# Attention scores of the first block: plain float32 products of 64 rows, or two float32r passes over 128 rows

## The chip, the cores and the metric

One core of a Trainium2 chip runs the whole program. The metric is device microseconds of one execution; the time of the kernel before is the median of three runs. TensorE multiplies, VectorE (DVE), ScalarE (ACT) and GpSimd (POOL) work on tiles of 128 partitions, and SyncE issues the loads of the weights.

## What is computed

Two stacks of layers over 256 rows of 1024 columns in float32. The first block has four layers: sliding-window attention (A), a mixture of three dilated attentions (B), an attention over the own block (C), and A again, each followed by a gated feed-forward net. The second block has two layers of another kind; its difference attention is computed as before. What the change touches is the score product of the first block, for one head:

```python
s = jnp.einsum('bnqhgd,bnkhd->bnhgqk', qb, kb) * (dh ** -0.5)   # dh = 64
s = jnp.where(ok[None, :, None, None], s, NEG)
m = s.max(-1)
p = jnp.exp(s - m[..., None])
o = jnp.einsum('bnhgqk,bnkhd->bnqhgd', p, vb) / ...
```

Layer A has 16 query heads on 4 key heads, layers B (three times, once for each dilation) and C have 16 query heads on 16 key heads.

## The kernel before

The 256 rows are two row tiles, t=0 and t=1, and each is a stream of work of its own: a Python generator that runs through all layers. The two take turns, the second four turns behind the first (LAG, line 54). A turn of a stream is half a unit of weights, which is six large products of 128x128 weights with 512 columns (mm3, line 399): inputs and weights are each split into a high and a low float32r part, and high-high, high-low and low-high are summed. ScalarE makes the high part of a weight and VectorE the low one (load, line 373), into eight buffers that both streams read. Beside a stream run small tasks, up to three a turn (spawn and turn, lines 430 and 438), among them the attention of four heads at a time. A scheduler of the framework then fixes the order of the instructions on each engine, and TensorE and the others follow that order.

A projection of 512 columns gives two blocks of 256, which are keys, values or queries of four heads (after, line 751). Keys and queries get the rotary step on VectorE (rope_apply, line 568), and then heads_t (line 580): two transposes of 128x128 into one PSUM bank and one eviction by ScalarE into a tile of 128 partitions by 2 x 128, two heads in the two halves of the partitions. In layer A each key head is first copied twice side by side (line 705), so that it lies in both halves, which makes four transposes and two evictions. In layer B the blocks come in the order v, k, q for each quarter and dilation, two to a chunk, so in every second group keys and queries come from one chunk.

scores (line 598) takes two PSUM banks, one for each parity of the four heads, and makes one plain float32 product with 64 rows for every head and 128 keys: four for t=0, which sees 128 keys, eight for t=1, which sees 256. The parities alternate. VectorE then adds the mask in PSUM and finds the maximum, ScalarE takes the exponential (attend, line 618), the probabilities are transposed (p_t, line 650) and multiplied with v. PSUM banks are named by tags: pj (3) for projections, ch (3) for scores and outputs, tp (2) for transposes. The tile v of a group is filled by ScalarE after a POOL memset of its column of ones (line 590); there are 7 buffers for v, 5 for keys (kt) and 3 for queries (qt).

Of the kernel before, what the change touches and what calls it, by code (L numbers as in the profile page):

```python
# [9 lines left out]
F32 = mybir.dt.float32  # L10
# [33 lines left out]
            bc=3, bcs=1, v=7, kt=5, qt=3, stg1=2, og=7, ob=3, ffg=4,  # L44
# [40 lines left out]
class Net:  # L85
# [45 lines left out]
    def own(self, name, shape, tag, dt=F32):  # L131
# [3 lines left out]
        pp = self.pl if tag in ("ho", "wx", "yt") else self.pp  # L135
# [462 lines left out]
    def scores(self, t, q, k, mask):  # L598

        nc = self.nc
        nk = (t + 1) * P
        svs = [self.bank().rearrange("p (h k) -> p h k", k=256)[:, :, :nk] for _ in range(2)]
        for a in range(2):
            for j in range(t + 1):
                for par in range(2):
                    nc.tensor.matmul(svs[par][:, a, j * P:(j + 1) * P], q(par, a), k(par, a, j), start=True, stop=True)  # L608
        for sv in svs:
# [3 lines left out]
            else:  # L613
                m = mask[:, None, (1 - t) * P:].to_broadcast([P, 2, nk])
                nc.vector.tensor_add(sv, sv, m)
        return svs

    def attend(self, t, qt, kt, mask, v, sink=None):
# [7 lines left out]
        svs = self.scores(t, lambda par, a: qt[par * 64:par * 64 + 64, a, :],  # L626
                          lambda par, a, j: kt(j, par + 2 * a), mask)
# [51 lines left out]
    def mixer_a(self, t, i, xt, st):  # L679
# [13 lines left out]
        def keys(ps):  # L693
# [7 lines left out]

            k2 = []
            for a in range(2):
                k = self.own("k2", [2, 2, 64], "stg1")
                nc.vector.tensor_copy(k, z[:, 128 * a:128 * a + 128].rearrange("p (h d) -> p h d", d=64)[:, :, None, :]
                                      .to_broadcast([P, 2, 2, 64]))
                k2.append(k.rearrange("p h a d -> p (h a d)"))
            yield from self.idle(W_QK_A)
            st["k", t] = [self.heads_t(k, "kt", 1.0) for k in k2]

        def queries(c, ps):
# [8 lines left out]
            qts = [self.heads_t(z, "qt", 0.125) for z in zs]  # L720
            yield
            def head(a):
                kvh = 2 * c + a
                h0 = 4 * kvh
                while ("k", 0) not in st:
                    yield
                o, nm = yield from self.attend(
                    t, qts[a], lambda jj, h: st["k", jj][kvh // 2][(h % 2) * 64:(h % 2) * 64 + 64, kvh % 2, :],
# [14 lines left out]
    def mixer_bc(self, t, i, xt, st, blocks, masks):  # L743
# [7 lines left out]
        def after(bl, ps):  # L751
# [20 lines left out]
            for zt, qq, g in qs:  # L772
                while any((a, qq, g, j) not in st for a in "kv" for j in range(t + 1)):
                    yield
# [741 lines left out]
```

## Time and profile before

| | |
|---|---|
| median of three runs | 2399.34 us (2399.07 to 2400.11) |
| the profiled execution | 2399.64 us |
| its span, first to last instruction | 2397.9 us |
| TensorE busy | 2357.5 us, 98% |
| VectorE, ScalarE, POOL busy | 1740.0, 1316.7, 150.3 us |

The span is read by stages. Attention of the four layers of the first block lies at about 35 to 110, 310 to 610, 820 to 925 and 1135 to 1215 us; the second block begins at about 1405 us.

### The profile page before, as it was taken

What the parts mean: (1) busy time and instruction counts of PE and PEld (TensorE: products, weight loads), DVE (VectorE), ACT (ScalarE), POOL (GpSimd) and SP (SyncE); (2) the same over time, 40 slices, a digit from 0 to 9 for tenths busy, and PEclk for the clock granted to TensorE, in tenths of its full rate; (3) what the DMA queues carried; (4) which work ended last, traced back from release to release, by engine and by line L of the source; (5) the groups of instructions that cost most, each with busy time, mean ns of one, the idle gap of its engine ahead of it and who ended that gap; (6) DMA issues with size and microseconds to landing.
All of it is one profiled execution on the core that took longest, in us unless ns stands there. A gap on an engine that the chain in (4) does not pass through costs nothing.

```text
span 2397.9 us, 34993 instructions
## 1 busy us (share of the span) xinstructions
PE 2357.5 (98%) x11664; PEld 1920.7 (80%) x11664; DVE 1740.0 (73%) x4260; ACT 1316.7 (55%) x2182; POOL 150.3 (6%) x433
## 2 busy tenths in 40 slices
PE   8999999999999999999999999999999999999999
PEld 6788878888788788887778877877888778788887
DVE  7755676666755767557775588987877889887876
ACT  5544456655444555444544445744677656545775
POOL 1100000000100001000010000100011201000111
PEclk9999999999999999999999999999999999999999
DMA  6366554444566645665366667567566686575663
GB/s 233 114 186 187 182 167 132 139 126 132 172 188 185 187 130 169 187 186 183 124 186 186 186 140 168 136 146 200 164 194 185 167 186 130 123 214 172 187 183 115
DMA packets 280117, 400.16 MB, mean 167 GB/s; under 512 B 20588, under 2 KB 205098, under 8 KB 279936
## 3 DMA queue, kind: packets, MB, share of 16 engines
q1 hardware_dynamic: 274784, 381.88, 55.2%
q0 software_dynamic: 5152, 16.05, 2.2%
q8 instruction: 92, 1.51, 0.3%
q14 instruction: 89, 0.73, 0.1%
HBM read 396.81 MB, written 1.05 MB: 166 GB/s over the span
## 4 chain that ended last, share of the span: by engine, by line
PE 86%; DVE 8%; DMA 3%; ACT 2%; issue 1%; ACTq 0%; DVEq 0%; SPq 0%
PE pj L404 21%; PE pj L406 21%; PE pj L405 21%; PE tp L451 4%; PE ch L404 4%; PE ch L406 4%; PE ch L405 4%; PE ch L608 3%; PE ch L646 2%; DVE w L395 2%; DMA raw<-in_w_in_dram 2%; PE tp L658 1%; ACT w L392 1%; DVE convy L997 1%; DVE x L545 0%
## 5 line engine op out<-in xcount | busy, mean ns | idle before, releaser
L395 DVE TENSOR_TENSOR w<-raw,w 128x512 fp32r<-128x512 f32 x1434 | 941.9, 683 | 467.2 <-ACT w L392 464.1
L392 ACT CAST w<-raw 128x1024 fp32r<-128x1024 f32 x728 | 758.9, 1043 | 659.8 <-PE pj L406 375.2
L404 PE MATMUL pj<-w,xth 128*128 128x512 f32 x2048 | 821.3, 402 | 4.9 <-DVE stg L716 1.9
L405 PE MATMUL pj<-w,xth 128*128 128x512 f32 x2048 | 804.0, 393 | 1.6 <-DVE w L395 1.5
L406 PE MATMUL pj<-w,xtl 128*128 128x512 f32 x2048 | 803.3, 393 | 1.6 <-DVE xtl L443 1.6
L404 PEld LDWEIGHTS pj<-w,xth 128*128 128x128 f32 x2048 | 385.7, 188 | 89.6 <-ACT xth L442 6.1
L406 PEld LDWEIGHTS pj<-w,xtl 128*128 128x128 f32 x2048 | 385.2, 188 | 86.3 <-DVE xtl L443 4.2
L405 PEld LDWEIGHTS pj<-w,xth 128*128 128x128 f32 x2048 | 386.1, 189 | 78.3 <-DVE w L395 4.1
L404 PE MATMUL ch<-w,fht 128*128 128x512 f32 x412 | 171.9, 417 | 1.8 <-ACT fht L442 1.8
L406 PE MATMUL ch<-w,fht 128*128 128x512 f32 x412 | 161.9, 393 | 0.0
L405 PE MATMUL ch<-w,fht 128*128 128x512 f32 x412 | 161.2, 391 | 0.0
L997 DVE SCALAR_TENSOR_TENSOR convy<-xc,ffn_cw,convy 128x128 f32<-128x128 f32 x352 | 100.7, 346 | 7.2 <-POOL ffn_hist L988 2.1
L406 PEld LDWEIGHTS ch<-w,fht 128*128 128x128 f32 x412 | 77.3, 188 | 18.4 <-DVE fht L443 0.8
L404 PEld LDWEIGHTS ch<-w,fht 128*128 128x128 f32 x412 | 77.4, 188 | 15.5 <-ACT fht L442 3.9
L405 PEld LDWEIGHTS ch<-w,fht 128*128 128x128 f32 x412 | 77.9, 189 | 12.2
L635 ACT ACTIVATE pexp<-ch,nm 128x128 f32<-128x128 f32 (+1 forms) x192 | 65.8, 421 | 38.2 <-DVE nm L630 23.9
L839 ACT ACTIVATE ffg<-pj 128x256 f32<-128x256 f32 x88 | 33.8, 384 | 86.0 <-PE pj L406 86.0
L994 ACT ACTIVATE convy<-xc,ffn_cw 128x128 f32<-128x128 f32 x176 | 72.8, 484 | 1.4
L646 PEld LDWEIGHTS ch<-v,pt 128*128 128x128 f32 x576 | 70.5, 191 | 2.9
L404 PE MATMUL pj<-w,fht 128*128 128x512 f32 x180 | 71.3, 396 | 0.0
L406 PE MATMUL pj<-w,fht 128*128 128x512 f32 x180 | 70.7, 393 | 0.0
L405 PE MATMUL pj<-w,fht 128*128 128x512 f32 x180 | 70.1, 389 | 0.0
(339 smaller groups left out, 2745.9 us busy)
## 6 DMA issues: line engine op xcount, KB each, us to landing
raw<-in_w_gate_up_dram SPq DMA_DIRECT2D x352, 256.0 KB, 3.3
raw<-in_w_in_dram SPq DMA_DIRECT2D x128, 512.0 KB, 5.0
raw<-in_w_down_dram SPq DMA_DIRECT2D x88, 512.0 KB, 3.6
raw<-in_ffn_w_up_dram SPq DMA_DIRECT2D x176, 256.0 KB, 3.3
raw<-in_b_w_qkv_dram SPq DMA_DIRECT2D x144, 256.0 KB, 3.1
raw<-in_ffn_w_down_dram SPq DMA_DIRECT2D x44, 512.0 KB, 4.5
raw<-in_a_w_qkv_dram SPq DMA_DIRECT2D x24, 512.0 KB, 4.5
raw<-in_c_w_qkv_dram SPq DMA_DIRECT2D x48, 256.0 KB, 3.3
```

The lines of the kernel that those rows point to most:

```text
L392: nc.scalar.copy(w[:, 0, :m], raw)
L395: self.last_low = e.tensor_sub(w[:, 1, s], raw[:, s], w[:, 0, s].bitcast(F32)).ins
L404: mm(ps, xh[:, k, :], wh[:, kk, cols], start=start, stop=False)
L405: mm(ps, xh[:, k, :], wl[:, kk, cols], start=False, stop=False)
L406: self.last_mm = mm(ps, xl[:, k, :], wh[:, kk, cols], start=False, stop=stop).ins
L451: self.nc.tensor.transpose(tp[:, b * P:(b + 1) * P], src[:, b * P:(b + 1) * P], self.ident)
L608: nc.tensor.matmul(svs[par][:, a, j * P:(j + 1) * P], q(par, a), k(par, a, j), start=True, stop=True)
L635: nc.scalar.activation(p[:, a, :(t + 1) * P], sv[:, a, :], AF.Exp, bias=n2[:, a:a + 1])
L646: nc.tensor.matmul(o[:, par + 2 * a, :], pts[par][:, a * (t + 1) + j, :], v(j, par + 2 * a), start=j == 0, stop=j == t)
L839: nc.scalar.activation(g, ps[:, :FFC], AF.Silu)
L994: nc.scalar.activation(y[:, a, :], xc[:, a, 4:], AF.Identity, bias=b[:, 0, c:c + 1], scale=w[:, h, c:c + 1])
L997: nc.vector.scalar_tensor_tensor(y[:, a, :], xc[:, a, o:o + P], w[:, j, c:c + 1], y[:, a, :], op0=OP.mult, op1=OP.add)
```

## The change

Queries and keys of the first block are now split into a high and a low float32r part too. For a head, the query tile holds its high part in the 64 partitions where the head's keys lie and its low part in the other 64, already scaled by 0.125 (queries_t). A key tile holds, for 256 keys of four heads, the high parts and the low parts, each in both halves of the partitions (keys_t): ScalarE writes the high part, VectorE the low one, and POOL copies both to the other half. A score is then the sum of two float32r products over all 128 rows, query tile with the high keys and query tile with the low keys, with 128 columns for t=0 and 256 for t=1. The parities come one after the other. One key tile holds both row tiles of a group, in two buffers; v gets 6 buffers for 7, and the doubled keys of layer A go. The second block's scores keep the old form under the name scores_64.

```diff
-            bc=3, bcs=1, v=7, kt=5, qt=3, stg1=2, og=7, ob=3, ffg=4,
+            bc=3, bcs=1, v=6, ks=2, qs=3, stg1=2, og=7, ob=3, ffg=4,
...
-    def heads_t(self, z, tag, scale):
-
+    def queries_t(self, z, scale):
+        nc = self.nc
         tp = self.blocks_t(z, 2)
-        zt = self.own("zt", [2, P], tag)
-        self.nc.scalar.activation(zt, tp, AF.Copy, scale=scale)
+        zt = self.own("zt", [2, 2, P], "qs", F32R)
+        for par in range(2):
+            here, there = self.half(par), self.half(1 - par)
+            nc.scalar.activation(zt[here, par], tp[here], AF.Copy, scale=scale)
+            nc.vector.scalar_tensor_tensor(zt[there, par], tp[here], scale, zt[here, par].bitcast(F32),
+                                           op0=OP.mult, op1=OP.subtract)
         return zt
+
+    def keys_t(self, z, ks, j):
+        nc = self.nc
+        tp = self.blocks_t(z, 2)
+        s = slice(j * P, (j + 1) * P)
+        for par in range(2):
+            here, there = self.half(par), self.half(1 - par)
+            nc.scalar.copy(ks[here, 0, par, :, s], tp[here])
+            nc.vector.tensor_sub(ks[here, 1, par, :, s], tp[here], ks[here, 0, par, :, s].bitcast(F32))
+            nc.gpsimd.tensor_copy(ks[there, :, par, :, s], ks[here, :, par, :, s])
+
+    def key_pair(self):
+        return self.own("ks", [2, 2, 2, 2 * P], "ks", F32R)
...
+    def scores(self, t, q, k, mask):
+        svs = self.score_banks(t)
+        for par, sv in enumerate(svs):
+            for a in range(2):
+                for part in range(2):
+                    self.nc.tensor.matmul(sv[:, a, :], q(par, a), k(par, a)[:, part, :(t + 1) * P],
+                                          start=part == 0, stop=part == 1)
+        return self.masked(t, svs, mask)
...
-            k2 = []
-            for a in range(2):
-                k = self.own("k2", [2, 2, 64], "stg1")
-                nc.vector.tensor_copy(k, z[:, 128 * a:128 * a + 128].rearrange("p (h d) -> p h d", d=64)[:, :, None, :]
-                                      .to_broadcast([P, 2, 2, 64]))
-                k2.append(k.rearrange("p h a d -> p (h a d)"))
             yield from self.idle(W_QK_A)
-            st["k", t] = [self.heads_t(k, "kt", 1.0) for k in k2]
+            self.keys_t(z, self.shared((i, "ks"), self.key_pair), t)
+            st["k", t] = True
...
-                    st["k", qq, g, t] = self.heads_t(z, "kt", 1.0)
+                    self.keys_t(z, self.shared((i, "ks", qq, g), self.key_pair), t)
+                    st["k", qq, g, t] = True
                 else:
-                    qs.append((self.heads_t(z, "qt", 0.125), qq, g))
+                    qs.append((self.queries_t(z, 0.125), qq, g))
```

## Rows read from the trace of the kernel before

**Rows 1.** The page's head: engine busy, share of the span, instructions.
```profile
span 2397.9 us, 34993 instructions
PE 2357.5 (98%) x11664; PEld 1920.7 (80%) x11664; DVE 1740.0 (73%) x4260; ACT 1316.7 (55%) x2182; POOL 150.3 (6%) x433
```

**Rows 2.** The page's chain that ended last, shares by engine.
```profile
PE 86%; DVE 8%; DMA 3%; ACT 2%; issue 1%; ACTq 0%; DVEq 0%; SPq 0%
```

**Rows 3.** Waits of TensorE: who waited <- releaser: us in total, times, longest.
```profile
PE pj L405 <- DVE w L395: 1.5, 2, 1.1
...
PE ch L608 <- ACT pexp L635: 0.2, 1, 0.2
```

**Rows 4.** Table by stage (layers B, C): stretch, busy us, granted clock, DMA.
```profile
310.00:600.00 290.00, 289.79 (x1690) 238.52 (x1689) 191.71 (x530) 171.60 (x369) 2.84 (x23) 1.00 0.45 138
820.00:920.00 100.00, 99.81 (x572) 82.34 (x573) 62.77 (x169) 59.10 (x119) 0.32 (x3) 1.00 0.47 145
```

**Rows 5.** Timeline, TensorE then VectorE, after a shared chunk: start, us, instruction [idle before].
```profile
353.99 0.61 PE L451 MATMUL tp<-ident,stg 128*128 128x128 f32 x4
...
354.67 0.39 PE L405 MATMUL pj<-w,xth 128*128 128x512 f32 x1
...
357.11 0.69 DVE L395 TENSOR_TENSOR w<-raw,w 128x512 fp32r<-128x512 f32 x1 [3.72 <-ACT w L392]
```

**Rows 6.** Timeline of TensorE around two score calls of t=1.
```profile
339.71 0.40 PE L406 MATMUL pj<-w,xtl 128*128 128x512 f32 x1
340.04 1.53 PE L608 MATMUL ch<-zt 64*128 64x128 f32 x16
...
341.83 0.39 PE L405 MATMUL pj<-w,xth 128*128 128x512 f32 x1
...
356.96 0.39 PE L406 MATMUL pj<-w,xtl 128*128 128x512 f32 x1
357.28 1.16 PE L608 MATMUL ch<-zt 64*128 64x128 f32 x16
...
358.71 0.39 PE L405 MATMUL pj<-w,xth 128*128 128x512 f32 x1
```

**Rows 7.** Lines and groups: counts, durations ns (min/median/max or mean), a wait.
```profile
L608 PE MATMUL ch<-zt x576: 272/272/373, 39.1 to 1196.8; 64*128 64x128 f32 x192
...
  ACT pexp L635: 3.7, 10
...
L451 PE MATMUL tp<-ident,k x16: 270/272/330, 25.0 to 1149.1; 128*128 128x128 f32 x16
...
L584 ACT ACTIVATE zt<-tp 128x256 f32<-128x256 f32 x88 | 32.1, 386 | 35.2 <-PE tp L451 33.5 <-PE ch L608 1.5 <-ACT zt L584 0.2
...
L443 DVE TENSOR_TENSOR fht<-tp,fht 128x256 fp32r<-128x256 f32 x104 | 43.4, 417 | 1.0 <-ACT fht L442 1.0
...
L442 ACT CAST fht<-tp 128x256 fp32r<-128x256 f32 x104 | 38.3, 368 | 10.0 <-PE tp L451 6.6 <-PE ch L406 1.9 <-PE pj L406 1.6
```

**Rows 8.** Timeline of TensorE around a score call of t=0.
```profile
323.59 0.40 PE L406 MATMUL pj<-w,xtl 128*128 128x512 f32 x1
323.92 0.71 PE L608 MATMUL ch<-zt 64*128 64x128 f32 x8
...
324.90 0.39 PE L405 MATMUL pj<-w,xth 128*128 128x512 f32 x1
```

**Rows 9.** Timeline of TensorE around four float32r products of 128 columns.
```profile
1576.13 0.40 PE L406 MATMUL pj<-w,xtl 128*128 128x512 f32 x1
1576.37 0.56 PE L1102 MATMUL ch<-ssact,pick 128*128 128x128 f32 x4
...
1577.04 0.40 PE L404 MATMUL pj<-w,xth 128*128 128x512 f32 x1
```

**Rows 10.** POOL's groups (busy, mean ns), and its waits from 310 to 600 us.
```profile
L395 POOL TENSOR_TENSOR w<-raw,w 128x512 fp32r<-128x512 f32 x22 | 28.6, 1319 | 553.0 <-ACT w L392 543.2 <-DVE eg L801 9.8
...
L166 POOL COPY maskt<-same 128x128 f32<-128x128 f32 x2 | 0.6, 289 | 50.7 <-DVE same L217 50.7
...
L278 POOL COPY r2cc<-r2cc 128x8 f32<-128x8 f32 x2 | 0.4, 184 | 0.4 <-ACT r2cc L277 0.4
...
POOL v L590 <- PE ch L646: 278.7, 16, 40.7
```

More of the change, by code (lines that the diff above doesn't have):

```diff
@@ L134, in own @@
             self.second_pool()
-        pp = self.pl if tag in ("ho", "wx", "yt") else self.pp
+        pp = self.pl if tag in ("ho", "wx", "ks", "yt") else self.pp
         return pp.tile([P] + shape, dt, name=name, tag=tag, bufs=BUFS[tag])
@@ L596, in v_tile, with masked @@
         return v
-    def scores(self, t, q, k, mask):
+    def masked(self, t, svs, mask):
         nc = self.nc
-        nk = (t + 1) * P
-        svs = [self.bank().rearrange("p (h k) -> p h k", k=256)[:, :, :nk] for _ in range(2)]
-        for a in range(2):
-            for j in range(t + 1):
-                for par in range(2):
-                    nc.tensor.matmul(svs[par][:, a, j * P:(j + 1) * P], q(par, a), k(par, a, j), start=True, stop=True)
         for sv in svs:
@@ L613, in scores, with score_banks, scores_64 @@
             else:
-                m = mask[:, None, (1 - t) * P:].to_broadcast([P, 2, nk])
+                m = mask[:, None, (1 - t) * P:].to_broadcast([P, 2, (t + 1) * P])
                 nc.vector.tensor_add(sv, sv, m)
         return svs
+    def score_banks(self, t):
+        return [self.bank().rearrange("p (h k) -> p h k", k=256)[:, :, :(t + 1) * P] for _ in range(2)]
+    def scores(self, t, q, k, mask):
[6 more added lines that the diff above has]
+        return self.masked(t, svs, mask)
+    def scores_64(self, t, q, k):
+        svs = self.score_banks(t)
+        for a in range(2):
+            for j in range(t + 1):
+                for par in range(2):
+                    self.nc.tensor.matmul(svs[par][:, a, j * P:(j + 1) * P], q(par, a), k(par, a, j),
+                                          start=True, stop=True)
+        return self.masked(t, svs, None)
     def attend(self, t, qt, kt, mask, v, sink=None):
@@ L624, in attend @@
         ps = []
-        svs = self.scores(t, lambda par, a: qt[par * 64:par * 64 + 64, a, :],
-                          lambda par, a, j: kt(j, par + 2 * a), mask)
+        svs = self.scores(t, lambda par, a: qt[:, par, a, :], lambda par, a: kt(par + 2 * a), mask)
         for par, sv in enumerate(svs):
@@ L719, in queries @@
             yield from self.idle(W_QK_A)
-            qts = [self.heads_t(z, "qt", 0.125) for z in zs]
+            qts = [self.queries_t(z, 0.125) for z in zs]
             yield
@@ L1138, in diff_attn @@
             ps, ls = [], []
-            svs = self.scores(t, lambda m, a: qt[64 * m:64 * m + 64, 2 * hp + a, :],
-                              lambda m, a, j: st["dk", j][64 * m:64 * m + 64, 2 * hp + a, :], None)
+            svs = self.scores_64(t, lambda m, a: qt[64 * m:64 * m + 64, 2 * hp + a, :],
+                                 lambda m, a, j: st["dk", j][64 * m:64 * m + 64, 2 * hp + a, :])
             for sv in svs:
```

10 lines of the change are left out of this document (7 added, 3 removed).

## The prediction

> **What bounds the kernel now.** I read the page's busy line and its chain first. TensorE is busy for 98% of a span of 2397.9 us [rows 1], and 86% of the chain that ended last is TensorE's own work [rows 2]. What TensorE waits for is small: of the waits that bear on this change the longest sum is 1.5 us, on the weights' low parts, and the scores wait 0.2 us in all [rows 3]. In the largest attention stage TensorE is busy 289.79 of 290 us, VectorE 191.71 and ScalarE 171.60, at a granted clock of 1.00 [rows 4]. So a saving counts here if it shortens what TensorE issues, and an addition on the other engines costs only where TensorE, which works in a fixed order, comes to wait for it.
>
> A busy TensorE overstates one instruction: records overlap. The unit is therefore what a burst inserts between the large products: from the start of the last 512-column product before it to the start of the second one after it, less two of their steps. Their step is 2.29 us for ten, from 354.67 to 356.96, so 0.229 us [rows 5, 6].
>
> **The price of the scores before.** The trace holds 576 records of score products in the first block [rows 7]; a plain float32 product leaves two, so these are 288 products: 24 calls for rows t=0 with 4 and 24 for t=1 with 8. A t=0 call inserts 324.90 - 323.59 - 0.458 = 0.85 us [rows 8]. A t=1 call inserts 358.71 - 356.96 - 0.458 = 1.29 us where nothing is late, and 341.83 - 339.71 - 0.458 = 1.66 us where it is [rows 6]. Eight more records thus cost 0.44 us, 0.055 us each, while eight alone cost 0.85: some 0.41 us of every call is entering and leaving. I read this as pairs that run beside each other in the two halves of the rows, with a toll at either edge. Both kinds of t=1 call are frequent, so I take the middle, 1.47 us, and keep both ends.
>
> **The price after.** Each call becomes 8 products over all 128 rows, t=0 with 128 columns and t=1 with 256. The nearest row is the second block's line 1102: four float32r products, 128 rows by 128 columns, insert 1577.04 - 1576.13 - 0.458 = 0.45 us, 0.113 each, with no toll [rows 9]. That also speaks against a penalty for a narrow float32r product: it costs half of a 512-column one. A t=0 call is then 8 x 0.113 = 0.90 us, 0.05 more than before: 24 x 0.05 = 1.2 us lost. For 256 columns there is no row. From below it is 0.113 (nothing cheaper than the narrow product), from above the straight line from 0.113 at 128 columns to 0.229 at 512, which is 0.152. Half of a 512-column step is 0.115; I take 0.12, near the low end, since 128 columns already cost more than a quarter of 512. A t=1 call is 8 x 0.12 = 0.96 us (0.90 to 1.22), and 24 x (1.47 - 0.96) = 12.2 us are won. With both sets of ends this term runs from 24 x (1.29 - 1.22) = 1.7 us to 24 x (1.66 - 0.90) = 18.2 us.
>
> The Trainium skill ("TensorE: Matmul & The Clock Gate", Back-to-back issue gap) gives about 81 ns for a sustained pair of weight load and 128-column product. By it a t=0 call would be an estimated 0.65 us and the sum 6 us better; the row of line 1102 shows 113 ns for this kernel's float32r form, and I go by the row.
>
> **Transposes.** The sliding-window layers no longer double their keys: 16 transposes of k [rows 7] become 8. At 0.113 us, the price of the narrow product (nearest row), this is 0.9 us won on TensorE, and eight copies go from VectorE.
>
> **What is added beside TensorE.** Key tiles: 2 x (1+12+4+1) = 36. Query tiles: 2 x (4+12+4+4) = 48. Before, 88 evictions of 386 ns served both [rows 7]. Now a key tile takes two ScalarE copies, two VectorE subtractions and two POOL copies, a query tile two ScalarE and two VectorE passes; every one has 64 partitions by 256 elements, POOL's 64 by 512. I price them by the 128-partition rows of the same length: 368 ns on ScalarE, 386 with a scale, 417 ns on VectorE [rows 7]. ScalarE: 72 x 0.368 + 96 x 0.386 - 88 x 0.386 = +29.6 us. VectorE: 168 x 0.417 = +70 us, less the eight copies. POOL: a copy of 128 elements takes 289 ns and one of 8 takes 184, so 512 elements are 184 + 504 x 0.875 = 625 ns; the far row is the two-operand 512-element subtraction at 1319 ns [rows 10]. 72 x 0.625 = 45 us.
>
> In the dilated stage 24 key tiles and 24 query tiles add 96 x 0.417 = 40 us to VectorE's 191.7 (80% of the stage) and some 18 us to ScalarE's 171.6 (65%) [rows 4]. Neither becomes the bound of the stage. As a load these are covered by TensorE; what matters is latency.
>
> **Latency, and who waits.** From a tile's transposes to its scores the way was one eviction. For keys it is now ScalarE, VectorE and POOL, and POOL serially for the two halves: 0.37 + 0.42 + 2 x 0.625 = 2.04 us, with handoffs some 2.2 us. The shortest cover is where keys and queries come from one chunk: transposes start at 353.99, the scores at 357.28 [rows 5, 6], 2.9 us after the last of four transposes. The second parity's scores come half a call later, 0.45 us more cover. VectorE is idle for 3.72 us there [rows 5], but it also has two query passes behind the key's two: 0.37 + 4 x 0.42 + handoffs = 2.3 us. So nothing is late where VectorE is free, and up to 0.7 us is late where a pair of weight subtractions (2 x 0.69 us) stands in front. On POOL the keys' copies stand behind the v tile's memsets, which wait for the attention product of an older group, 278.7 us in sum and up to 40.7 us at a time [rows 10]. With six v buffers for seven that wait ends one tile earlier in the ring; it harms only if the fixed order puts a key copy behind a memset whose release TensorE reaches after those scores. POOL's order follows TensorE's, so I put this at nothing, and at the price of the slower rival if not. Behind a late weight subtraction stand the large products; eight weight buffers cover that. The transposes' two PSUM banks are held longer, 0.37 + 2 x 0.42 us for 0.39; the trace shows the next transposes mostly 2 us or more behind.
>
> Exposed I count one VectorE pass, 0.42 us, at six places where TensorE has little else: the start of the first layer for both row tiles and the end of four attention stages, 2.5 us; none to 6 x 1.35 us (2.04 less two evictions shortened by the faster call) as its ends, 0 to 8 us.
>
> **Sum.** -12.2 + 1.2 - 0.9 + 2.5 = -9.4 us. The profiled execution took 2399.64 us, 1.74 more than its span and 0.3 more than the median of 2399.34. From the median: 2390 us. Its own range, by the ends: best -18.2 + 1.2 - 0.9 = -17.9, so 2381; worst -1.7 + 1.2 - 0.9 = -1.4 without exposures, so 2398; the 8 us of exposure on top of that is left to the rivals.
>
> **Rivals.** (1) The waits stay. The 0.37 us by which some t=1 calls are late stay late (1.29 is then the fair price before), and exposures are about 5 us: -24 x 0.33 + 1.2 - 0.9 + 5 = -2.6, 2397 us, within 0.2%. For it: what holds the scores' weight loads is mostly ScalarE's exponentials, 3.7 us in 10 waits [rows 7], and ScalarE gets more work. Against: the new order does one parity after the other, so the second bank is needed half a call later.
>
> (2) Slower: POOL's copies set the time of the scores. Price per same-chunk group (12 in the dilated layer): 0.37 + 0.42 + 2p + 0.2 less 2.9 + 0.45. It cancels the 11.9 us of TensorE when it reaches 1.0 us a group, at p = 1.7 us. At 2.0 us the stall is 1.6 x 12 = 20 us and the time 2399.3 - 11.9 + 20 = 2407 us. For it: no POOL copy of this size or between partitions is in the trace. Against: even the two-operand row, 1.32 us, is below that point.
>
> (3) Slower: giving up the pairs costs more than the toll gives. If the new calls also paid the 0.41 us at their edges, the sum would be 48 x 0.41 = 20 us worse: 2410 us. Against it stands line 1102, which pays none [rows 9]. The Trainium skill ("TensorEngine Tiling (Array Packing)", Overview and Key Properties) has both sides: small contractions gain up to 2x from row tiles, which is against this change, and switching the tiling mode drains the engine. The trace agrees with both: 0.055 us a record inside a call, 0.41 us around it.
>
> (4) It does more than it says. By its columns alone a 128-column product would be 0.229 / 4 = 0.057 us; if in a run of eight it costs the middle between that and 0.113, 0.085 us, t=0 calls give 24 x 8 x 0.028 = 5.4 us more: 2385 us. The four of line 1102 speak against it.
>
> **How the numbers follow.** Forecast 0.59, rival 1 0.23, rival 2 0.11, rival 3 0.04, rival 4 0.03. What a measurement can tell from no change is about 0.2%, 4.8 us. Faster: 0.59 + 0.03 = 0.62; same 0.23; slower 0.11 + 0.04 = 0.15. The range takes in the forecast's ends, rivals 1 and 4 and the beginning of rival 2: 2381 to 2404.
>
> **What would show it.** Right: no toll at the edges of score bursts, about 0.90 us for t=0 and 0.96 for t=1; POOL copies near 0.6 us; TensorE still at 98% with score waits of a few us in its list; VectorE near 80% in the dilated stage. Wrong: waits of the scores for POOL of 10 us or more (rival 2), bursts above 1.2 us that wait for nothing (rival 3), or waits for weights that grew, which would mean that VectorE's load was not covered.

## The result, and the profile after

| | before | after |
|---|---|---|
| median | 2399.4 us (2399.07 to 2400.11) | 2412.45 us (2409.34 to 2412.94) |
| ratio, 95% interval | | 1.0051 [1.0038, 1.0063] |
| the profiled execution, its span | 2399.64 us, 2397.9 us | 2412.7 us, 2411.0 us |
| TensorE, VectorE, ScalarE, POOL busy | 2357.5, 1740.0, 1316.7, 150.3 us | 2347.7, 1813.9, 1352.1, 204.3 us |

The change costs 13 us where the forecast said that it would give back 9. The page's head and the chain of after, against [rows 1, 2]:

```profile
span 2411.0 us, 34920 instructions
PE 2347.7 (97%) x11464; PEld 1924.1 (80%) x11464; DVE 1813.9 (75%) x4420; ACT 1352.1 (56%) x2265; POOL 204.3 (8%) x505
...
PE 82%; DVE 11%; ACT 3%; DMA 3%; issue 1%; SPq 0%; ACTq 0%; DVEq 0%
```

TensorE has 10 us less to do, as foreseen, but its share of the chain falls from 86% to 82% and VectorE's rises from 8% to 11%: TensorE waits more than it saves. The list of its waits says for whom (waiter <- releaser: us in total, times, longest; [rows 3] is the list before):

```profile
PE tp L451 <- DVE stg L578: 5.9, 12, 0.9
PE tp L451 <- DVE zt L590: 5.5, 12, 0.7
...
PE ch L646 <- DVE zt L590: 4.3, 7, 1.4
...
PE ch L646 <- ACT pexp L678: 2.0, 3, 1.4
...
PE ch L646 <- POOL ks L604: 1.1, 2, 0.5
```

The first line is transposes that wait for the rotation. The second is transposes that wait for a PSUM bank of tp, which VectorE's pass for the low part still reads. Before, the two came to 1.2 and 0.5 us:

```profile
PE tp L451 <- DVE stg L578: 1.2, 3, 0.8
PE tp L451 <- ACT zt L584: 0.5, 2, 0.3
```

The scores themselves (L646) wait 4.3 us for the low pass, and only 1.1 us for POOL. The two attention stages of [rows 4], with the same columns:

```profile
310.00:600.00 290.00, 284.11 (x1569) 238.61 (x1570) 233.90 (x623) 186.72 (x411) 37.05 (x68) 1.00 0.45 138
820.00:920.00 100.00, 97.27 (x525) 80.88 (x524) 78.24 (x211) 61.72 (x130) 12.22 (x22) 1.00 0.48 149
```

VectorE stands at 81% of the dilated stage, as forecast, and TensorE now idles 5.9 us of the 290, against 0.2. Not all of this comes from the passes: the products alone, in f1_products below, already leave it idle for 3.9 us of such a stretch, mostly for exponentials.

For the time by stage I cut the trace at the starts of the large products (512 columns), whose number, 8688, is the same in every kernel. The profiled execution of after against the one of before: first layer with its feed-forward net 268.7 us for 260.4, dilated layer 336.9 for 335.3, layer C 115.6 for 114.3, the attention of the second layer A 92.6 for 92.6, the second block with its start 2.1 us longer. So 8.3 of the 13 us lie in the first layer. There the granted clock falls to the lower level (1.2 GHz) three times, for 13.7 us together; before, it never did in that layer. A table by stretches around the longest of them, first after, then before (stretch, length, busy us of PE, PEld, DVE, ACT, POOL, granted clock):

```profile
60.00:64.80 4.80, 2.93 (x20) 2.02 (x18) 4.49 (x12) 3.34 (x8) 0.00 (x0) 1.00 0.32 77
64.90:71.50 6.60, 6.17 (x22) 5.36 (x23) 4.47 (x18) 3.05 (x10) 0.00 (x0) 0.50 0.06 21
```
```profile
60.00:64.80 4.80, 4.62 (x32) 3.30 (x31) 3.85 (x12) 2.75 (x8) 0.00 (x0) 1.00 0.35 111
64.90:71.50 6.60, 6.60 (x36) 5.21 (x35) 5.27 (x23) 4.24 (x10) 0.50 (x1) 1.00 0.00 0
```

After, TensorE is busy for 2.93 of the 4.80 us and then gets half its clock; before, it is busy for 4.62 and keeps it. Its gaps in that stretch of after (TensorE's timeline: start, us, instruction [idle before]):

```profile
61.13 0.41 PE L451 MATMUL tp<-ident,stg 128*128 128x128 f32 x2 [0.50 <-DVE zt L590]
62.31 0.41 PE L451 MATMUL tp<-ident,stg 128*128 128x128 f32 x2 [0.38 <-DVE zt L590]
63.88 0.41 PE L451 MATMUL tp<-ident,ob 128*128 128x128 f32 x2 [0.49 <-DVE zt L590]
65.33 0.80 PE L404 MATMUL pj<-w,ho 128*128 128x512 f32 x1 [1.03 <-ACT ho L442]
```

Three times transposes stand before a bank that VectorE has not let go. Ahead of the other two falls, at 44.3 and 88.7 us, the longest gaps are scores that wait for the low pass of their own queries:

```profile
41.63 0.63 PE L646 MATMUL ch<-ks,zt 128*128 128x128 f32 x4 [1.12 <-DVE zt L590]
...
88.20 0.84 PE L646 MATMUL ch<-ks,zt 128*128 128x256 f32 x4 [1.44 <-DVE zt L590]
```

In the three stretches at the lower level TensorE is busy nearly throughout (12.3 of 13.0 us in the windows that I read). At half the clock half of that time is lost, so I estimate their cost at about 6 of the 8.3 us; the rest I put down to the gaps.

The price of the products is as forecast. A score call of t=0 in after, to be read like [rows 8]:

```profile
477.52 0.39 PE L406 MATMUL pj<-w,xtl 128*128 128x512 f32 x1
477.75 1.00 PE L646 MATMUL ch<-ks,zt 128*128 128x128 f32 x8
478.60 0.44 PE L404 MATMUL pj<-w,xth 128*128 128x512 f32 x1
478.88 0.40 PE L405 MATMUL pj<-w,xth 128*128 128x512 f32 x1
```

It inserts 478.88 - 477.52 - 0.458 = 0.90 us, without a toll. And so are the passes, one by one (groups: busy us, mean ns of one):

```profile
L604 POOL CAST ks<-ks 64x512 fp32r<-64x512 f32 x72 | 52.9, 735 | 267.0 <-DVE ks L603 248.6 <-DVE ropea L575 14.2 <-DVE rl L710 2.7
L590 DVE SCALAR_TENSOR_TENSOR zt<-tp,zt 64x256 fp32r<-64x256 f32 x96 | 40.1, 421 | 10.2 <-ACT zt L589 7.5
L589 ACT ACTIVATE zt<-tp 64x256 fp32r<-64x256 f32 x96 | 35.6, 378 | 30.7 <-PE tp L451 18.6 <-DVE zt L590 11.1
```

ScalarE's line shows something that was not in the working: its pass for the second half waits 11.1 us for VectorE's pass on the first half.

### The profile page after: what moved, and what is told of

Its sections match the earlier page's. It is cut to its first block, busy times and chain, and to the rows that moved or that the text cites. A ratio compares the mean times of both kernels' runs of the same rounds, so it can differ in the third digit from the quotient of the medians.

```text
span 2411.0 us, 34920 instructions
## 1 busy us (share of the span) xinstructions
PE 2347.7 (97%) x11464; PEld 1924.1 (80%) x11464; DVE 1813.9 (75%) x4420; ACT 1352.1 (56%) x2265; POOL 204.3 (8%) x505
## 3 DMA queue, kind: packets, MB, share of 16 engines
q8 instruction: 90, 1.47, 0.3%
## 4 chain that ended last, share of the span: by engine, by line
PE 82%; DVE 11%; ACT 3%; DMA 3%; issue 1%; SPq 0%; ACTq 0%; DVEq 0%
PE pj L404 20%; PE pj L406 20%; PE pj L405 20%; PE tp L451 4%; PE ch L404 4%; PE ch L406 4%; PE ch L405 4%; DVE w L395 3%; PE ch L689 2%; ACT w L392 2%; PE tp L701 1%; PE ch L646 1%; DMA raw<-in_a_w_qkv_dram 1%; DVE zt L590 1%; DMA raw<-in_w_in_dram 1%
## 5 line engine op out<-in xcount | busy, mean ns | idle before, releaser
L451 PE MATMUL tp<-ident,stg 128*128 128x128 f32 x424 | 69.5, 275 | 9.9 <-DVE stg L578 5.9
L604 POOL CAST ks<-ks 64x512 fp32r<-64x512 f32 x72 | 52.9, 735 | 267.0 <-DVE ks L603 248.6
L395 POOL TENSOR_TENSOR w<-raw,w 128x512 fp32r<-128x512 f32 x22 | 29.5, 1361 | 511.9 <-ACT w L392 504.8
```

The lines of the kernel that those rows point to most:

```text
L395: self.last_low = e.tensor_sub(w[:, 1, s], raw[:, s], w[:, 0, s].bitcast(F32)).ins
L451: self.nc.tensor.transpose(tp[:, b * P:(b + 1) * P], src[:, b * P:(b + 1) * P], self.ident)
L604: nc.gpsimd.tensor_copy(ks[there, :, par, :, s], ks[here, :, par, :, s])
```

## The experiments

The ratios are to the kernel before, run beside each kernel (its medians there: 2398.9 to 2400.0 us). One thing must be kept in mind in all of them: the framework's scheduler places the instructions anew when passes are added or taken away. I compared TensorE's order in the records. It is the same in the second block of all kernels compared; in the first block it is the same in the pairs that are named as such below, and differs a little in the others.

### Where the loss lies

**e5_a_old**: the old form in the sliding-window layers, the new one in the others.

```diff
-            self.keys_t(z, self.shared((i, "ks"), self.key_pair), t)
+            st["k", t] = [self.heads_t(k, 1.0, ks[:, t, a]) for a, k in enumerate(k2)]
...
-            qts = [self.queries_t(z, 0.125) for z in zs]
+            qts = [self.heads_t(z, 0.125) for z in zs]
```

> The changed kernel with layers A (first and fourth) in the old form: doubled keys, one eviction, 64-row float32 scores, in the buffers of the new kernel; layers B and C in the new form. The traces put 8.5 of the 13 us of loss into the first layer. Theory A with the clock (the first layer has VectorE 89% busy from 30 to 60 us already, so late passes idle TensorE there and its clock falls to half three times): 2401 to 2406 us, no half clock between 30 and 110 us. If the loss is spread by a rearranged order and moves elsewhere: 2408 us or more.

Measured: 2400.82 us, 1.0006 [0.9997, 1.0016]. The first layer is 0.9 us shorter than before, the dilated one and C are 1.3 us longer each.

**f2_a_alone**: the reverse, the new form in the sliding-window layers alone.

```diff
-                    self.keys_t(z, self.shared((i, "ks", qq, g), self.key_pair), t)
+                    st["k", qq, g, t] = self.heads_t(z, 1.0, "kt")
...
-                    qs.append((self.queries_t(z, 0.125), qq, g))
+                    qs.append((self.heads_t(z, 0.125, "qt"), qq, g))
```

> The mirror of the run with the sliding-window layers in their old form: they alone get the new form, the other two attention layers keep the old one. Theory D: the loss sits in the first layer, so nearly all of it returns: 2407 to 2412 us, first layer 6 to 10 us longer than before, dilated stage within 2 us of before. Theory A (late passes everywhere): 2402 to 2405 us, since the larger number of calls (24 of 48 or more) is outside these layers.

Measured: 2408.33 us, 1.0038 [1.0023, 1.0053]; first layer 5.9 us longer than before, with 10.2 us at the lower clock. The second block, whose order is the same, is 4.6 us longer in this execution, so not all of the time lies where the change is. Within the first block the loss comes with layer A, and in the other two layers, with 32 of the 48 score calls, nothing is won either (e5_a_old).

**e7_v6**: the kernel before with v=6 for v=7, the one buffer that the change takes.

> The kernel before with six buffers for v in place of seven, the one part of the change that adds no work. Theory A: no effect, 2398 to 2401 us. Theory D (any other order): an effect only if the order in the first layers moves; then 2402 to 2408 us with half clock between 30 and 110 us.

Measured: 2401.19 us, 1.0004 [0.9995, 1.0013], TensorE's order unchanged. By itself, the buffer costs nothing that could be told from no change.

### One kind of pass taken away

**e2_no_dve**: no VectorE pass; the low halves of the tiles are zeroed once.

```diff
             nc.scalar.activation(zt[here, par], tp[here], AF.Copy, scale=scale)
-            nc.vector.scalar_tensor_tensor(zt[there, par], tp[here], scale, ...)
...
-            nc.vector.tensor_sub(ks[here, 1, par, :, s], tp[here], ...)
```

> The changed kernel with all 168 new VectorE passes left out: the low halves of query and key tiles stay zero in fixed tiles (three for queries, two for keys, as many as the rings had), so the low parts are not computed; ScalarE's passes, POOL's copies and the score products stay. Theory A (VectorE comes late: its in-order queue makes scores and transposes wait, and in the first layer the idle time drops TensorE's clock): all of the loss goes and the cheaper scores show, 2388 to 2395 us, no stretch at half clock between 30 and 110 us. Theory B (POOL's copies set the time of the scores): still 2406 us or more. Theory C (the new products are no cheaper than the old ones in place): 2400 to 2405 us, with score bursts as in the changed kernel and TensorE idle as before.

Measured: 2408.6 us, 1.0033 [1.0019, 1.0048]. Only 4 us of the 13 return. In the dilated stage TensorE still idles 7 us: for exponentials and, though VectorE is back at 199 us there, for the rotation (2.9 us). That VectorE's passes alone were the cause is refuted.

**e3_no_pool**: no POOL copies, so that half of each score's sum is missing. TensorE's order is that of the changed kernel.

```diff
-            nc.gpsimd.tensor_copy(ks[there, :, par, :, s], ks[here, :, par, :, s])
```

> The changed kernel with the 72 POOL copies left out: the other half of each key tile stays zero in fixed tiles, so half of each score's sum is missing; ScalarE's and VectorE's passes and the score products stay. Theory A (VectorE late): little changes, 2408 to 2413 us. Theory B (POOL's copies): 2390 to 2400 us.

Measured: 2407.72 us, 1.0033 [1.0020, 1.0046]. About 4.7 us return, four times the 1.1 us that the scores waited for POOL.

**e1_order**: of each tile, both ScalarE passes first, then VectorE's, then POOL's.

> The changed kernel with the same passes in another order: for each tile first both ScalarE passes, then both VectorE passes, then (keys) both POOL copies, where the changed kernel goes half by half. Its trace shows ScalarE waiting for the VectorE pass of the first half before its own second pass (19 times, 11.1 us for queries, 16 times, 9.4 us for keys). Theory A (ScalarE and VectorE in turns make the chain late, and ScalarE's queue with it): those waits vanish and the time falls to 2400 to 2406 us. Theory D (in the first layer TensorE has little to fill with; any other fixed order opens gaps there and the clock falls to half): no clear gain, 2406 to 2414 us, stretches at half clock between 30 and 110 us stay, in other places.

Measured: 2411.9 us, 1.0050 [1.0033, 1.0067], no change in the total. In the profiled execution the loss has moved: the first layer is 2.4 us longer than before, for 8.3 in the changed kernel, but the second layer A 3.4 us, for none, and the second block 3.8. So it is not shown that ScalarE's wait for VectorE within a tile costs nothing, only that removing it gains nothing in all.

### The products alone, and the passes put back one kind at a time

**f1_products**: one ScalarE eviction per tile, as before, and nothing else beside the new products; the low parts are left out of the result.

```diff
-        for par in range(2):
...
+        nc.scalar.activation(zt[:, 0], tp, AF.Copy, scale=scale)
...
+        nc.scalar.copy(ks[:, 0, 0, :, s], tp)
```

> Only the products change against the kernel before: the new scores, one ScalarE eviction of all 128 partitions per tile as before, no VectorE and no POOL pass; queries and keys lie in tiles whose other part was zeroed once, so the low parts are left out of the result. Theory A (the added passes make the scores late): without them the products' saving shows whole, about 8 us of TensorE with waits gone, 2391 us, and the first layer is no longer than before. Theory D (the first layer's order is tight, and any other order there opens gaps and half-clock stretches): 2402 to 2408 us, with the first layer still 3 to 8 us longer than before; the dilated stage at most 3 us shorter. Theory P (the products themselves were overpriced before): no gain in the dilated stage either, 2400 us or more there and everywhere.

Measured: 2395.01 us, 0.9980 [0.9969, 0.9991], faster than before. In its profiled execution the first layer is 0.5 us shorter than before, the dilated one 4.6, C 0.5, the second layer A 2.8: some 8 us in the first block with its start. (Of the 4.6 us, 1.1 come at the end of the stage, where the kernel before has 3.4 us at the lower clock and this one none.) The second block, with the same order of instructions, is 4.9 us longer, at the lower clock for 17.0 us against 3.4. A call of t=1 here, which the changed kernel seldom has in one piece (TensorE's timeline, as in [rows 6]):

```profile
356.77 0.39 PE L407 MATMUL pj<-w,xtl 128*128 128x512 f32 x1
357.00 1.11 PE L648 MATMUL ch<-ks,zt 128*128 128x256 f32 x8
357.95 0.39 PE L405 MATMUL pj<-w,xth 128*128 128x512 f32 x1
358.18 0.40 PE L406 MATMUL pj<-w,xth 128*128 128x512 f32 x1
```

It inserts 358.18 - 356.77 - 0.458 = 0.95 us; the forecast said 0.96. But the calls that were late before are not cheaper. The one that inserted 1.66 us in [rows 6] is here:

```profile
339.48 0.39 PE L407 MATMUL pj<-w,xtl 128*128 128x512 f32 x1
339.71 0.63 PE L648 MATMUL ch<-ks,zt 128*128 128x256 f32 x4
340.84 0.74 PE L648 MATMUL ch<-ks,zt 128*128 128x256 f32 x4 [0.49 <-ACT pexp L680]
...
341.64 0.40 PE L406 MATMUL pj<-w,xth 128*128 128x512 f32 x1
```

It inserts 341.64 - 339.48 - 0.458 = 1.70 us, 0.49 of them idle, and the two others that inserted 1.66 (at 436 and 484 us) insert 1.70 and 1.71. So a call that waits for nothing costs what the prediction said. Against this run, the passes that make the operands cost 2412.45 - 2395.01 = 17.4 us, together with the order that comes with them.

**g2_beside**: the products as in f1_products, and all added passes beside them, into tiles that no product reads. (Here and in the next three, both products of a score read the same part of the keys, and the low parts are left out of the result.)

```diff
         nc.scalar.activation(zt[:, 0], tp, AF.Copy, scale=scale)
...
+        nc.scalar.activation(self.own("more", [2, P], "more", F32R)[there], tp[there], AF.Copy, scale=scale)
+        for par in range(2):
+            here = self.half(par)
+            nc.vector.scalar_tensor_tensor(low[here], tp[here], scale, zt[here, 0].bitcast(F32), ...)
...
+            nc.gpsimd.tensor_copy(twice[there], ks[here, 0, :, :, s])
```

> The new products with one whole ScalarE eviction per tile as in the run of the products alone, and the added work put back beside it: per tile a second ScalarE pass and two VectorE passes, per key tile two POOL copies, all of the sizes of the changed kernel, into tiles that no product reads; the low parts are left out of the result. If the loss is latency (scores that wait for these passes): within 3 us of the products alone, 2392 to 2398 us, and the dilated stage as short as there, 331 us. If it is load (other work delayed on VectorE and ScalarE, banks of the transposes held longer): near the changed kernel, 2405 to 2412 us, dilated stage 336 us or more.

Measured: 2414.09 us, 1.0064 [1.0049, 1.0079]. The whole loss is back though no score waits for VectorE's passes or POOL's. So the longer way from a transpose to its scores is not needed for a loss of this size; what the passes do to other work, with the order that comes with them, is enough. But the loss does not lie in the same places: in the profiled execution the first layer is 3.5 us longer than before, for 8.3 in the changed kernel, and the second layer A 5.0 us, for none. In the first layer the longer way may well have its part. TensorE's waits in the dilated stage (318 to 608 us), first of f1_products, then of g2_beside:

```profile
PE ch L648 <- ACT pexp L680: 3.5, 6, 0.7
PE tp L452 <- DVE stg L579: 0.2, 1, 0.2
```
```profile
PE tp L452 <- DVE stg L579: 2.5, 4, 1.0
PE tp L452 <- ACT w L393: 2.2, 3, 0.8
PE tp L452 <- DVE rl L729: 1.8, 2, 0.9
PE ch L665 <- ACT pexp L697: 1.7, 3, 0.6
```

With the passes, transposes come to wait for the rotation and the normalisation, which stand behind them on VectorE.

**h1_act, h2_dve, h3_pool**: of these passes those of one engine alone, ScalarE's second, VectorE's two, POOL's two.

> The products alone (low parts left out of the result), and per tile ScalarE's second pass back, into a tile that no product reads. If ScalarE's 84 more passes delay the projection's evictions and with them the rotation and the transposes: 2401 to 2406 us, with 4 us or more of TensorE gaps in the dilated stage, most of them in transposes that wait for the rotation. If VectorE's load does it: within 3 us of the products alone, 2393 to 2398 us.

> The products alone (low parts left out of the result), and per tile VectorE's two passes back, into a tile that no product reads. If VectorE's 70 us do it, by holding up the rotation: 2402 to 2408 us, with 4 us or more of TensorE gaps in the dilated stage. If ScalarE's second pass does it: 2393 to 2399 us, dilated stage 331 to 333 us.

> The products alone (low parts left out of the result), and per key tile POOL's two copies back, into a tile that no product reads. Both theories: POOL feeds nothing else that is tight, 2393 to 2398 us. If its copies slow VectorE or hold up the v tiles' memsets: 2400 us or more.

| passes beside the products | time, us | ratio to before | over the products alone |
|---|---|---|---|
| none (f1_products) | 2395.01 | 0.9980 [0.9969, 0.9991] | |
| POOL's (h3_pool) | 2401.49 | 1.0012 [1.0002, 1.0022] | 6.5 |
| VectorE's (h2_dve) | 2404.59 | 1.0024 [1.0014, 1.0033] | 9.6 |
| ScalarE's (h1_act) | 2405.97 | 1.0028 [1.0019, 1.0037] | 11.0 |
| all (g2_beside) | 2414.09 | 1.0064 [1.0049, 1.0079] | 19.1 |
| all, and read by the products (the change) | 2412.45 | 1.0051 [1.0038, 1.0063] | 17.4 |

Beside these products no engine's load is covered: any one of the three takes back the whole gain. (Which of the three costs more is hardly clear of the intervals.) I had expected one of ScalarE and VectorE to be harmless and POOL to be free, and all three were wrong on that. The single costs add up to 27 us for 19 together, so removing one returns little, as e2_no_dve and e3_no_pool had shown. Where they act, in TensorE's waits of the dilated stage, h1_act, h2_dve and h3_pool in turn:

```profile
PE ch L652 <- ACT pexp L684: 4.3, 5, 1.1
PE tp L452 <- DVE stg L579: 1.5, 6, 0.3
```
```profile
PE tp L452 <- DVE stg L579: 3.9, 7, 1.0
PE ch L657 <- ACT pexp L689: 0.9, 4, 0.3
```
```profile
PE tp L452 <- DVE stg L579: 4.4, 7, 0.7
PE ch L652 <- ACT pexp L684: 2.4, 6, 0.6
```

The products alone wait 3.5 us for exponentials and 0.2 for the rotation there. ScalarE's passes add 0.8 us for the exponentials and 1.3 for the rotation, VectorE's add 3.7 for the rotation and take 2.6 from the exponentials, POOL's add 4.2 for the rotation and take 1.1. In all TensorE idles 3.9 us of that stretch with the products alone, 6.3, 4.7 and 6.9 with one kind of pass, and 8.7 with all. In the first layer of h2_dve, transposes also wait 3.2 us in 4 waits for the bank that the low pass reads. POOL's case is the cleanest, since TensorE's order is exactly that of f1_products, and it is the strangest, since POOL's copies feed nothing here. VectorE, which has the same work as in f1_products, is busy for 1755.3 us in place of 1741.3. Its rotation in the dilated stage, first of f1_products, then of h3_pool (count | busy us, mean ns of one):

```profile
L576 DVE TENSOR_TENSOR ropea<-stg,r1cc 128x64 f32<-128x64 f32 x47 | 10.4, 221 | 16.9 <-ACT stg L799 16.5
L578 DVE TENSOR_TENSOR ropeb<-stg,r1ss 128x32 f32<-128x32 f32 x47 | 8.7, 185 | 0.0
```
```profile
L576 DVE TENSOR_TENSOR ropea<-stg,r1cc 128x64 f32<-128x64 f32 x47 | 14.1, 300 | 16.4 <-ACT stg L803 16.0
L578 DVE TENSOR_TENSOR ropeb<-stg,r1ss 128x32 f32<-128x32 f32 x47 | 12.1, 257 | 0.0
```

The same instructions take longer. One of the places in the timeline of h3_pool (POOL, VectorE, then TensorE):

```profile
337.22 1.77 POOL L601 CAST twice<-ks 64x512 fp32r<-64x512 f32 x2 [10.83 <-ACT ks L597]
...
337.78 0.63 DVE L576 TENSOR_TENSOR ropea<-stg,r1cc 128x64 f32<-128x64 f32 x1
338.33 0.18 DVE L577 TENSOR_TENSOR ropeb<-stg,r1ss 128x32 f32<-128x32 f32 x1
338.44 0.60 DVE L578 TENSOR_TENSOR ropeb<-stg,r1ss 128x32 f32<-128x32 f32 x1
...
339.51 0.41 PE L452 MATMUL tp<-ident,stg 128*128 128x128 f32 x2 [0.69 <-DVE stg L579]
```

A multiplication of 0.22 us takes 0.63 and one of 0.18 takes 0.60 while POOL copies, and TensorE waits 0.69 us for the result. The Trainium skill ("SBUF — State Buffer", Who interferes with whom) has the rule: a VectorE instruction with two inputs from SBUF contends with a GpSimd instruction that reads SBUF, for a shared port that only one of them can hold. The trace agrees: in the changed kernel the 20 low passes of queries that overlap a POOL copy, with one input in PSUM, take 421 ns in the mean, like the 76 that don't. In the changed kernel itself such long multiplications are few, 3 of 276 against 20 of 276 in h3_pool, and VectorE is busy for only 4.1 us more than in e3_no_pool (1813.9 for 1809.8), so the lock explains this run better than it explains the 4.7 us of e3_no_pool.

### Order alone

**e4_dve_beside**: the kernel before, with two VectorE passes per tile added that no product reads.

```diff
         self.nc.scalar.activation(zt, tp, AF.Copy, scale=scale)
+        low = self.own("low", [2, P], "low", F32R)
+        for par in range(2):
+            here = slice(64 * par, 64 * par + 64)
+            self.nc.vector.scalar_tensor_tensor(low[here], tp[here], scale, zt[here], op0=OP.mult, op1=OP.subtract)
```

> The kernel before with two VectorE passes of 64 partitions by 256 elements after each of its 88 evictions of transposed keys and queries (176 passes, 74 us), written to a scratch tile that nobody reads; scores as before. They lengthen no chain to the scores, but they stand in VectorE's queue and hold the transposes' PSUM bank. Theory A as load (what else stands in VectorE's queue comes late, and the bank is held): 2404 to 2412 us, TensorE's waits for VectorE grow. Theory A as chain (only the way from transposes to scores counts): 2399 to 2403 us. Theories B and C: 2399 to 2403 us.

Measured: 2408.11 us, 1.0038 [1.0023, 1.0052]. VectorE's passes cost the old form about as much (8.6 us) as they cost the new products in h2_dve. But the dilated layer, with VectorE at 80% of the stage, is 4.1 us shorter than before, and TensorE waits there for the rotation no more than before:

```profile
PE tp L451 <- DVE stg L578: 0.2, 1, 0.2
```

Of the 4.1 us, 1.3 come at the stage's end, where this kernel misses the 3.4 us at the lower clock of the kernel before; the other 2.8 come earlier, with another order, and were not followed. The loss lies in the two layers A and in C. So at the same share of VectorE the dilated stage covers these passes beside the old products, and not beside the new ones.

**e8_before_wait**: the kernel before with W_QK_A = 2 for 1; the transposes of layers A come one step later, and no work is added.

> The kernel before with one more idle turn between the rotary step and the transposes of queries and keys in layers A (the constant W_QK_A 2 in place of 1): not one instruction more or less, only another order around the first and the fourth layer. Theory A: about no effect, 2398 to 2402 us. Theory D: 2403 to 2410 us, gaps and half clock in the first layer.

Measured: 2408.19 us, 1.0039 [1.0024, 1.0054]: 4.7 us of it in the first layer, with 6.8 us at the lower clock. A different order there, with nothing added, costs as much as a kind of pass.

**e6_later**: the changed kernel with one more step between transposes and scores in all layers.

```diff
             yield
+            yield
             for zt, qq, g in qs:
```

> The changed kernel with the scores issued one turn later (one more yield between the queries' passes and the scores, in all four layers), so that six more large products of each stream lie between transposes and scores. Theory A (scores wait for the longer chain): the dilated layer gains 3 to 5 us and the time is 2402 to 2408 us. Theory D: layers with enough filler (dilated) gain, the first layer, with three chunks in all, does not or loses: 2408 to 2416 us.

Measured: 2428.81 us, 1.0122 [1.0107, 1.0138]. The loss is everywhere in the first block: 7.5 us more than before in the first layer, 7.2 in the dilated one, 7.5 in C and at its end, 5.9 in the second layer A. That later scores push the softmax and all behind it into thinner cover is my reading; it was not tried apart.

**f4_a_old_wait**: e5_a_old with W_QK_B = 1 for 0.

> Sliding-window layers in the old form, the other two in the new one, and in these the transposes come one step later, so that the rotation and the evictions of the projection are done when they are due. If the 4.8 us that TensorE idles more in the dilated stage are the transposes' wait for the rotation and the passes behind it, most of it is covered: 2395 to 2398 us, below both kernels. If the later transposes push softmax and attention products into what follows, 2401 to 2412 us.

Measured: 2408.75 us, 1.0037 [1.0024, 1.0050]; dilated layer 6.1 us longer than before, and 4.7 us more where layer C goes over into its feed-forward net. The second outcome came.

### Cover before the scores

**f3_earlier**: the changed kernel whole, W_QK_A = 0 for 1 and one more step before the scores of layers A: the transposes and all passes come one step earlier, the scores where they were.

> The changed kernel whole, but in the sliding-window layers the transposes are issued one step earlier and the scores stay where they are, so the longer way from transposes to scores has one more step of cover; all added work stays. Theory A: the waits of the scores and of the second ScalarE pass for VectorE in the first layer are covered, and the time comes down to 2402 to 2405 us. Theory D: another order in the same tight layer, so the gaps move to the transposes' wait for the rotation or to the softmax; within 4 us of the changed kernel, 2408 to 2416 us.

Measured: 2403.82 us, 1.0019 [1.0009, 1.0029]. 8.6 us return with all work in: the first layer is as long as before (1.0 us shorter, behind a start that is 1.1 us longer) and at the lower clock for 3.4 us, the second layer A 2.2 us shorter, the dilated one and C as in the changed kernel (+1.7 and +1.3, same order). The wait of transposes for the low pass falls from 5.5 us to 1.9, that of the scores from 4.3 to 1.1. So there is time for the passes on the engines of these layers, if they come early enough. This run has another order too, and e8_before_wait shows how much an order alone can move; how much of the 8.6 us is cover and how much is order stays open.

**g1_a_earlier**: the same for f2_a_alone.

> New form in the sliding-window layers alone, with their transposes one step earlier and their scores in place; the other two layers in the old form. If one more step of cover is what these layers lacked: first layer 1 us shorter than before, the fourth layer 2 us, the rest as before: 2395 to 2398 us, the first version with all its work that is not slower than the kernel before. If the order in the first layer decides by chance: 2402 to 2410 us.

Measured: 2399.83 us, 1.0003 [0.9994, 1.0013]; first layer with its start 3.1 us longer than before, the second layer A 2.4 us shorter. Neither outcome: no loss any more, and no gain.

**g3_earlier_order**: f3_earlier with the order of e1_order.

> The changed kernel with the transposes of the sliding-window layers one step earlier, and in all layers a tile's two ScalarE passes first, then the two VectorE passes, then the two POOL copies, so that ScalarE waits for VectorE no more between its two. If ScalarE's wait for VectorE within a tile is part of the latency: 2 to 5 us less than with the earlier transposes alone, 2398 to 2402 us. If VectorE's second pass decides by itself: no change, 2403 to 2406 us.

Measured: 2405.12 us, 1.0025 [1.0013, 1.0038], no better than f3_earlier. No version with all its work beat the kernel before.

## Why the prediction was wrong, step by step

**The products: right in their price, mis-sized in what they save.** 0.90 us for t=0 and 0.95 for t=1 were measured for 0.90 and 0.96, the toll is gone, and rival 3 falls with it. The saving was smaller than 11.9 us: some 8 us in the first block of f1_products, 4.4 us in its median over all. I had taken 1.47 us for the old t=1 call, the middle between undisturbed and late calls; the late ones stayed late, as rival 1 said, at 1.70 us for 1.66. With 1.29 for the old call the term is 24 x (1.29 - 0.95) = 8.2 us in place of 12.2, and with the other two 8.2 - 1.2 + 0.9 = 7.9 us. By that term alone the forecast would still have been a gain.

**The cost of each pass: right.** 421 and 420 ns on VectorE for 417, 378 and 367 on ScalarE for 386 and 368, some 611 undisturbed and 735 in the mean on POOL for 625. VectorE's share of the dilated stage was right too.

**"As a load these are covered by TensorE": the step that failed.** I compared each engine's busy time with the stage, found 80% and 65%, and called the load covered. But the engines work in a fixed order, and TensorE's transposes and softmax products wait for single passes of ScalarE and VectorE: beside the new products each kind of pass alone cost 6.5 to 11.0 us, though no product read what it made. The sign that I had named for uncovered load, waits for weights, hardly came (2.3 us on the low parts, for 1.5 before); it was the transposes that waited. I read it so: a pass of 0.4 us that stands ahead of a rotation can delay the rotation by 0.4 us at any busy share. In the kernel before such waits were almost none [rows 3], which I took for slack; that in the layers A it was an order with little to spare is what e8_before_wait suggests. The busy share misleads in the other direction too: in e4_dve_beside the dilated stage covers VectorE's passes at the same 80%, beside the old products. Why the new ones leave less cover there was not tried; TensorE idles 3.9 us beside them before any pass is added.

**Exposure: mis-sized.** I counted the passes only on the way from a tile's transposes to its own scores, at six places: 2.5 us, ends 0 to 8. The waits that I meant, those of scores for VectorE's low pass and for POOL, came to 4.3 + 1.1 = 5.4 us, within these ends. But the passes cost 17.4 us in all, order included, and 19.1 in the run in which no score waits for them. The mechanism was too narrow: what I should have asked is who stands behind each pass on its engine, at all 84 tiles, and what a gap does to the clock.

**The banks: dismissed wrongly.** I had noted that the transposes' two banks would be held for 0.37 + 2 x 0.42 us for 0.39, and that the next transposes come mostly 2 us later. They come sooner where it matters: 5.5 us of waits in 12 places, for 0.5 us in 2 before, three of them ahead of the longest stretch at the lower clock.

**Rival 2, POOL: the sign without the mechanism.** The scores waited 1.1 us for POOL, so its copies don't set the scores' time. They cost 6.5 us beside the products and 4.7 us in the change all the same, in one part by blocking VectorE.

**The clock: absent.** I took the granted clock for 1.00 in the first layer, since it was so before. Of the 8.3 us there about 6 are, by my estimate, the lower level, and ahead of each of the three stretches TensorE waits for a low pass.

**Open.** For POOL's copies the order of TensorE was the same with and without, so their cost is theirs. For ScalarE's and VectorE's passes the scheduler's order changed with them a little, and the runs don't divide the 11.0 and 9.6 us between the delay and the new order. In the changed kernel, the part of the first layer's loss that comes from the longer way to the scores is not divided from the rest. The second block, with the same order in all kernels, went in the profiled executions from 0.6 us shorter than before (e4_dve_beside) to 4.9 us longer (f1_products), and was longest where it had most time at the lower clock; what sets that was not tried, and it is as large as some of the effects above.

## What to carry to other kernels

Where one engine is busy for 98% by a fixed order, price an added pass on another engine by what is queued behind it and by the banks and buffers that it holds, not by the busy share of its engine alone. Run the saving alone, without what makes its operands, first: here that one run gave its worth, 4 to 5 us, against which 17 us of passes stood. If passes must come, try an earlier step for them before anything else; here that returned 8.6 us, and taking away a whole kind of pass only 4 to 5.

## What was not expected of the hardware

- In h3_pool, VectorE multiplications with both inputs in SBUF took 0.60 to 0.63 us beside POOL's copies of 64 partitions by 512 elements, for 0.18 to 0.22; in the changed kernel, VectorE passes with one input in PSUM kept their 421 ns beside such copies.
- float32r products of 128 rows cost 0.95 / 8 = 0.119 us at 256 columns (f1_products) and 0.90 / 8 = 0.112 at 128 (the changed kernel): almost the same price for twice the columns. At 512 columns the step is 0.229.
- The time of one and the same program follows its mean granted clock: ten executions of f1_products took 2391.5 us at 0.997 and 2404.7 us at 0.992 at the ends. At the lower level (1.2 GHz), TensorE's 512-column products in the first layer of the changed kernel follow each other at 0.43 us instead of 0.23.
